# A reordered weave in a two-layer diffusion backbone: side work set at other places among the projections

## The chip, the cores and the metric

One core of a Trainium2 chip runs the whole program. The metric is device time in microseconds, the median of several executions.

## The reference

Two layers work on 512 latent tokens and 256 context tokens of width 1024, all in float32. Cut to what matters:

```python
for l in range(2):
    hl = rms_norm(xl, norm1_g[l]) * (1 + sc1) + sh1        # sh1, sc1, ... from silu(c) @ ada_w (adaLN)
    p = h @ w_in[l]                                        # one wide projection, split into parts
    att = window_attention(rope(q), rope(k), v, kc, vc, sink)
    mls = mlstm_output(mlstm_bidir(...), o_pre, ml_g)      # 4 heads, chunks of 128, both directions
    hy  = hyena_operator(dwconv(u), hyena_filters(...))    # filters: two sine layers; two long convolutions
    y   = sum(sigmoid(gate_r) * (branch_r @ w_branch[r]) for r in range(3)) @ w_out[l]
    xl  = xl + g1 * y
    xl  = xl + g2 * conv_ffn(rms_norm(xl, norm2_g[l]) * (1 + sc2) + sh2)   # D_FF 2816, width-3 conv, SiLU gate
    # the context tokens go the same way in layer 0 only
return rms_norm(xl, final_g)
```

## The kernel before, in words

All activations are kept with channels on the 128 partitions and tokens along the row; a part is the 512 latent columns or the 256 context columns. Each float32 product is made of three: weights and activations are split into a high and a low half (`split`, L340: ScalarE casts the high half, VectorE subtracts to get the low half), and `kstep` (L404) issues high x high, high x low and low x high into one PSUM tile. A weight tile of 128x1024 comes by a DMA from SP's queue (`raw`, L391) and is split (`weight`, L396); there are four slots for raw tiles and three for each split half (`WB = (4, 3)`). `proj` (L421) is one unit: a weight tile against all eight k-blocks of the normalised activations `hlh`, `hll`.

The projections are the backbone. Between their k-steps, `tick` (L358) gives each lane a credit: the planner's cost of the k-step times the lane's rate. A lane is a Python generator that emits a few instructions and yields their cost; it is stepped while its credit is positive. So the yields and the rates (`RATE`, one set a layer) decide where in the program a side step stands among the projections. `finish` (L379) runs what is left of the lanes at the end of a stage, with no projections between. The framework then orders each engine's queue by priority, which is program order unless `high_priority` or `manual_schedule` says otherwise, and by when it expects operands; every engine takes its queue in that order.

Stages of a layer, each with its own pools of tiles (`SIZES`: so many wide T tiles, so many 512-column H tiles):
- A: the first three projections (`proj_first`, L425), the mLSTM gate projection, then branch gates (`gate_proj`, L1530; `NG1` says up to which). Lanes: in layer 0 the hyena filters (`filters`, L627: per length two sine layers, `sin_of` L607, then taps and their transform), the mLSTM gate scans (`ml_gates`, L1287). In layer 0 `start` (L1681) comes first: DMAs of the input, adaLN products, the norm of the latent half; TensorE keeps program order there.
- mix: attention projections, then mLSTM projections (`ml_proj`, L1231) with the attention lane (`att_mix`, L1083), then the hyena projections (`hy_proj`, L895, which write `hyd` to DRAM) with the mLSTM lane (`ml_mix`, L1390: per head `prep`, L1400, and `chain`, L1430, whose last part normalises a head, transposes it (L1512) and stores it).
- E: the remaining gates and the merges (L1564), with the hyena lane (`hy_mix`, L957). `hy_start` (L974) reads channels of `hyd` back, folds them (`fold`, L904: DMA, then VectorE's sum L913 and difference L914), transposes them (`fold_tok`, L918, line L924) and splits them. `hy_body` (L989) runs the two convolutions of a half of the channels, kt by kt: load a spectrum tile `g` (L1012), products `pu` (L1020), `pair_products` (L927), accumulation (L1038, L1045). The x1 channels are folded at its beginning; the next half's start is stepped in the second convolution.
- ffn: the out-projection (`out_proj`, L1599; its last `NTAIL` units run part by part), a norm, up projections in threes at first, then pairs, and a down projection (`down`, L1620) one chunk behind; `residual` (L1592, executed at L1595) adds into x. The norm of the second part is put into `deferred` and emitted by `run_deferred` (L451). `KEEP` says how many units of the last but one down projection wait until the last up projections are out.

adaLN vectors that are needed later come from the lane `ada_rows` (L516), two VectorE products a row block at L528 for layer 0.

## Time and profile before

| | us |
|---|---|
| median of three runs | 2725.51 (2724.69 to 2727.54) |
| the profiled execution | 2729.28 |
| its span | 2727.2 |
| TensorE matmuls busy | 2584.6 |
| VectorE busy | 1860.9 |
| ScalarE busy | 1040.8 |
| GpSimd busy | 249.3 |

The span runs from the first to the last instruction of the profiled execution. Matmuls are pipelined, so a matmul's own duration is longer than its share of the queue; what counts is whether TensorE stands still. The stages by time: A of layer 0 up to about 303 us, attention to 540, mLSTM to 690, hyena and merges to 983, out-projection and FFN to 1640; layer 1: A to 1765, attention to 1985, mLSTM to 2100, hyena and merges to 2300, then the out-projection, the FFN and the final norm.

### The profile page before, as it was taken

Reading aid. Unit: us, or ns where it says so; the run is one execution under the profiler, and the core shown is the slowest. Engines: PE = TensorE matmul, PEld = TensorE weight load, DVE = VectorE, ACT = ScalarE, POOL = GpSimd, SP = SyncE. Lnnn points to the kernel's source line nnn. Section 1 sums busy time; section 2 is a strip of 40 time slices with the busy share of each in tenths; the row PEclk is TensorE's granted clock in tenths of the full one; section 3 lists DMA queues with packets and bytes.
Section 4 is the critical chain, followed back from the end, with each engine's and each line's share of the span. In section 5 each row is a group of like instructions: output and inputs, shape, how many; then the busy total and the mean of one; then the engine's idle time right before and its main releaser. Section 6 shows DMA issues by size and latency. Waiting matters only on the chain. (4 is left out here: it accounts for less than half of the span.)

```text
span 2727.2 us, 37870 instructions
## 1 busy us (share of the span) xinstructions
PE 2584.6 (95%) x14434; PEld 2192.3 (80%) x14434; DVE 1860.9 (68%) x3349; ACT 1040.8 (38%) x1875; POOL 249.3 (9%) x277
## 2 busy tenths in 40 slices
PE   6998999999998898999999998999998989999998
PEld 2887888788887787888888887877887778888887
DVE  6775676687568756877877667766376577666656
ACT  5344344455222224433333235444354233533333
POOL 3221110000000201110110001310000002000000
PEclk9999999999999798999999999999999999999999
DMA  7434532323557431334433225553335565233331
GB/s 265 122 118 129 163 102 70 91 94 112 190 175 273 146 109 45 116 118 113 113 117 106 77 59 196 181 132 99 92 123 177 182 211 187 78 93 101 93 101 62
DMA packets 155461, 349.99 MB, mean 128 GB/s; under 512 B 15809, under 2 KB 53166, under 8 KB 155152
## 3 DMA queue, kind: packets, MB, share of 16 engines
q1 hardware_dynamic: 135280, 322.18, 36.7%
q0 software_dynamic: 20000, 25.40, 3.9%
q8 instruction: 114, 1.87, 0.3%
q14 instruction: 67, 0.55, 0.1%
HBM read 288.59 MB, written 52.17 MB: 125 GB/s over the span
## 5 line engine op out<-in xcount | busy, mean ns | idle before, releaser
L407 PE MATMUL pg<-hh,wh 128*128 128x512 f32 (+1 forms) x2536 | 919.1, 363 | 12.7 <-ACT hh L342 7.7
L407 PE MATMUL pg<-hlo,wh 128*128 128x512 f32 (+1 forms) x2536 | 904.4, 357 | 2.7 <-DVE hlo L343 2.6
L407 PE MATMUL pg<-hh,wl 128*128 128x512 f32 (+1 forms) x2536 | 901.7, 356 | 0.1
L407 PEld LDWEIGHTS pg<-hh,wh 128*128 128x128 f32 x2536 | 485.5, 192 | 79.6 <-ACT hh L342 8.7
L342 ACT CAST wh<-wr 128x1024 fp32r<-128x1024 f32 x294 | 308.8, 1051 | 614.2 <-PE pg L407 580.4
L407 PEld LDWEIGHTS pg<-hlo,wh 128*128 128x128 f32 x2536 | 485.4, 191 | 64.8 <-DVE hlo L343 4.5
L407 PEld LDWEIGHTS pg<-hh,wl 128*128 128x128 f32 x2536 | 484.2, 191 | 65.3 <-issue 2.1
L343 DVE TENSOR_TENSOR wl<-wr,wh 128x1024 fp32r<-128x1024 f32 x294 | 363.6, 1238 | 204.5 <-ACT wh L342 200.1
L1595 DVE SCALAR_TENSOR_TENSOR x<-pg,mod,x 128x512 f32<-128x512 f32 (+1 forms) x242 | 148.9, 629 | 103.7 <-PE pg L407 96.5
L407 PE MATMUL pg<-fh,wh 128*128 128x512 f32 (+1 forms) x544 | 193.6, 357 | 11.2 <-DVE x L1595 10.5
L407 PE MATMUL pg<-fl,wh 128*128 128x512 f32 (+1 forms) x544 | 191.2, 352 | 0.0
L407 PE MATMUL pg<-fh,wl 128*128 128x512 f32 (+1 forms) x544 | 190.2, 350 | 0.9 <-DVE wl L343 0.9
L806 ACT ACTIVATE u<-pg,sv 128x512 f32<-128x512 f32 (+1 forms) x165 | 116.3, 707 | 122.5 <-PE pg L407 122.4
L807 DVE SCALAR_TENSOR_TENSOR u<-pg,sv,u 128x511 f32<-128x511 f32 (+1 forms) x165 | 108.4, 659 | 73.4 <-ACT u L806 72.8
L528 DVE SCALAR_TENSOR_TENSOR wr<-wr,silb 128x1024 f32<-128x1024 f32 x80 | 100.1, 1252 | 40.0 <-DMA wr<-in_adat 39.5
L407 PEld LDWEIGHTS pg<-fh,wh 128*128 128x128 f32 x544 | 103.4, 190 | 28.8 <-DVE x L1595 13.2
L407 PE MATMUL pg<-bh,wh 128*128 128x512 f32 (+1 forms) x320 | 114.5, 389 | 4.4 <-ACT bh L342 3.8
L407 PEld LDWEIGHTS pg<-fh,wl 128*128 128x128 f32 x544 | 103.4, 190 | 15.2 <-DVE wl L343 1.4
L407 PEld LDWEIGHTS pg<-fl,wh 128*128 128x128 f32 x544 | 103.6, 191 | 14.3 <-issue 0.7
L808 DVE SCALAR_TENSOR_TENSOR u<-pg,sv,u 128x511 f32<-128x511 f32 (+1 forms) x165 | 108.6, 660 | 2.2
L1136 ACT ACTIVATE p<-s,sm 128x512 f32<-128x512 f32 (+2 forms) x80 | 55.2, 690 | 127.6 <-DVE sm L1133 97.4
L407 PE MATMUL pg<-bh,wl 128*128 128x512 f32 (+1 forms) x256 | 97.2, 380 | 0.0
(321 smaller groups left out, 4043.9 us busy)
## 6 DMA issues: line engine op xcount, KB each, us to landing
wr<-in_wA SPq DMA_DIRECT2D x222, 512.0 KB
wr<-in_adat SPq DMA_DIRECT2D x80, 512.0 KB
wr<-in_wD SPq DMA_DIRECT2D x48, 512.0 KB
wr<-in_wB SPq DMA_DIRECT2D x24, 512.0 KB
gates<-gt SPq DMA_DIRECT2D x28, 384.0 KB
gc<-in_g POOLq DMA_DIRECT2D x40, 256.0 KB, 3.2
g<-gd SPq DMA_DIRECT2D x40, 256.0 KB
g<-gates SPq DMA_DIRECT2D x24, 384.0 KB
```

Of the source, the lines that this page charges most:

```text
L342: nc.scalar.copy(h, src)
L343: (nc.gpsimd if pool else nc.vector).tensor_tensor(l, src, h.bitcast(F32), op=ALU.subtract)
L407: self.nc.tensor.matmul(ps[:, :hi - lo], a[:, ks], b[:, lo:hi], start=(first and i == 0), stop=(last and i == 2))
L528: nc.vector.scalar_tensor_tensor(prod, aw, 1.0, self.silb[:, v, :], op0=ALU.mult, op1=ALU.mult, accum_out=self.mod[l][:, b * 4 + c, v:v + 1])
L806: nc.scalar.activation(dst[:, lo:hi], ps[:, :n], AF.Identity, bias=b, scale=w(1))
L807: V(dst[:, lo + 1:hi], ps[:, 0:n - 1], w(0), dst[:, lo + 1:hi], op0=mul, op1=add)
L808: V(dst[:, lo:hi - 1], ps[:, 1:n], w(2), dst[:, lo:hi - 1], op0=mul, op1=add)
L1136: nc.scalar.activation(t[:, :w], src, AF.Exp, bias=sm[:, 2 + j:3 + j], scale=0.125, accum_out=sm[:, 4 + j:5 + j])
L1595: self.nc.vector.scalar_tensor_tensor(x[m][:, lo:hi], ps[:, :hi - lo], self.mod[l][:, p * 8 + m, j:j + 1], x[m][:, lo:hi], op0=ALU.mult, o ...
```

## The change

- `filters` loses its sine layers to a generator `features`, which steps both lengths in turn. In layer 0 its first ten steps are emitted ahead of everything at high priority, two more behind the first adaLN product, the rest behind the first half of the norm; the filter lane is spawned after the eighth k-step of the first projections (`START` goes).
- `chain` ends with the last recurrence; the rest of a head becomes `tail`, which `ml_mix` steps at every even step of the next head's chain. The last tail yields its costs twice.
- `hy_start` folds the x1 channels too, for all halves before the first transposes, and yields 8.0 behind the folds at the beginning and 0.5 otherwise (2.0 before); the next start is stepped at the end of the first convolution as well. The E pool gets a 28th H tile.
- `att_mix` yields 4.0 before its first item.
- `NTAIL` 2 to 3; in the FFN `run_deferred` is called after k-step 3 (layer 0) or 1 (layer 1) of the first part (`MID`); the first three projections always go k by k together.
- `KEEP` of layer 0 goes from 0 to 4, `NG1` of layer 1 from 11 to 13, the adaLN lane of layer 0 from 1/12 to 1/8; rates of layer 1: mlg 0.616 to 0.7, att 1.008 to 0.84, ml 2.5 to 1.75, hy 2.149 to 1.1.

```diff
--- before.py
+++ after.py
@@ -240,22 +240,22 @@
 
 
 class Prog:
-    NG1 = (18, 11)
+    NG1 = (18, 13)
     NG2 = (18, 16)
-    RATE = ({'filt': 1.587, 'ada': 1.362, 'mlg': 0.55, 'att': 0.92, 'ml': 1.258, 'hy': 0.997}, {'filt': 0.389, 'ada': 0.512, 'mlg': 0.616, 'att': 1.008, 'ml': 2.5, 'hy': 2.149})
-    SIZES = {'A0': (18, 23), 'A1': (8, 38), 'mix': (20, 19), 'E': (16, 27), 'ffn0': (20, 21), 'ffn1': (28, 0)}
+    RATE = ({'filt': 1.587, 'ada': 1.362, 'mlg': 0.55, 'att': 0.92, 'ml': 1.258, 'hy': 0.997}, {'filt': 0.389, 'ada': 0.512, 'mlg': 0.7, 'att': 0.84, 'ml': 1.75, 'hy': 1.1})
+    SIZES = {'A0': (18, 23), 'A1': (8, 38), 'mix': (20, 19), 'E': (16, 28), 'ffn0': (20, 21), 'ffn1': (28, 0)}
     BOUNDS = ((0, 2, 4, 6, 8, 10, 12, 14, 16, 18, 22), (0, 4, 8, 12, 16, 20, 22))
-    START = (0.8,)
     FILL = (6.0, 6.0, 6.0)
     SQP = ((), (0, 1, 2, 3, 4, 5, 6, 7))
     AHEAD = 50
     EARLY = True
-    KEEP = (0, 2)
+    KEEP = (4, 2)
+    MID = (3, 1)
     TAKE = 50
     FADDS = 7
     WB = (4, 3)
     FINP = (1, 4)
-    NTAIL = 2
+    NTAIL = 3
@@ -294,7 +294,7 @@
         self.A = {(l, i): c.tile([P, KD, 2], F32, name=f"A{l}{i}") for l in range(DEPTH) for i in (1, 2)}
         self.sil = c.tile([P, KD, 32], F32, name="sil")
         self.silb = c.tile([P, 2, D], F32, name="silb")
-        self.g_dram = {}
+        self.g_dram, self.feat = {}, {}
 
     def load_consts(self):
         nc, a = self.nc, self.a
@@ -422,9 +422,12 @@
         w = self.weight(self.a["wA"][l, m])
         return list(self.gemm(w, 0, self.hlh, self.hll, parts))
 
-    def proj_first(self, l, ms, parts, hooks=None):
-
-
+    def proj_first(self, l, ms, parts, hooks=None, mid=None):
+
+
+        hooks = dict(hooks or {})
+        if mid is not None:
+            hooks[mid] = self.run_deferred
         raws = self.early or [None] * 3
         self.early = None
         ws = [self.weight(self.a["wA"][l, m], raw=r) for m, r in zip(ms, raws)]
@@ -433,15 +436,15 @@
             one = [self.G() for _ in ms]
         outs = [[] for _ in ms]
         for i, (lo, hi, _) in enumerate(parts):
-            if i:
+            if i and mid is None:
                 self.run_deferred()
             pss = [ps[:, lo:hi] for ps in one] if joint else [self.G() if i == 0 else self.M() for _ in ms]
-            for group in ((0,), (1,), (2,)) if i else ((0, 1, 2),) if hooks else ((0, 1), (2,)):
+            for group in ((0,), (1,), (2,)) if i else ((0, 1, 2),):
                 for k in range(KD):
                     for j in group:
                         self.kstep(pss[j], ws[j], slice(k * P, k * P + P), self.hlh[k], self.hll[k], lo, hi, k == 0, k == KD - 1)
                     self.tick(3 * len(group) * max(0.109, (hi - lo) * 0.422e-3))
-                    if i == 0 and hooks and k in hooks:
+                    if i == 0 and k in hooks:
                         hooks[k]()
             for o, ps in zip(outs, pss):
                 o.append((lo, hi, ps))
@@ -451,8 +454,8 @@
     def run_deferred(self):
         for f in self.deferred:
             f()
-        for rate, gen in self.late:
-            self.spawn(rate, gen)
+        for rate, *gens in self.late:
+            self.spawn(rate, *gens)
         self.deferred, self.late = [], []
 
     def parts(self, l, ctx=None):
@@ -624,17 +627,25 @@
         nc.scalar.activation(out, a, AF.Sin)
         yield 1.0
 
-    def filters(self, l, L, resident, overlap):
-
+    def features(self, l, lengths):
+
+        gens = [self.feature(l, L) for L in lengths]
+        while gens:
+            for g in list(gens):
+                c = next(g, None)
+                if c is None:
+                    gens.remove(g)
+                else:
+                    yield c
+
+    def feature(self, l, L):
         nc, a = self.nc, self.a
         s = "5" if L == SEQ else "2"
-        nT = L // P
         zt = self.H("zt")
         nc.sync.dma_start(zt[0:33, :L], a["z" + s])
         w12 = self.H("w12")
         nc.sync.dma_start(w12[0:33, 0:64], a["hw1"][l])
         nc.sync.dma_start(w12[0:64, P:2 * P], a["hw2"][l])
-        dec, gc = {}, {}
         h = zt
         yield 0.1
         for i, (kk, m) in enumerate(((33, 64), (64, P))):
@@ -649,7 +660,15 @@
         nc.scalar.copy(hd[0:64, :L], h[0:64, :L])
         nc.vector.tensor_tensor(hd[64:128, :L], h[64:128, :L], hh[64:128, :L].bitcast(F32), op=ALU.subtract)
         yield 1.5
-        dec = {}
+        self.feat[l, L] = hd
+
+    def filters(self, l, L, resident, overlap):
+
+        nc, a = self.nc, self.a
+        s = "5" if L == SEQ else "2"
+        nT = L // P
+        hd = self.feat[l, L]
+        dec, gc = {}, {}
         if resident:
             for t in range(nT):
                 dec[t] = self.H("dec")
@@ -959,9 +978,10 @@
 
         need = l < DEPTH - 1
         st = {}
-        yield from self.hy_start(l, SEQ, (0,), st)
-        yield from self.hy_body(l, SEQ, 0, st, out, self.hy_start(l, SEQ, (1,), st))
-        yield from self.hy_body(l, SEQ, 1, st, out, self.hy_start(l, CTX, (0, 1), st) if need else iter(()))
+        for c in self.hy_start(l, SEQ, (0,), st, 8.0):
+            yield c
+        yield from self.hy_body(l, SEQ, 0, st, out, self.hy_start(l, SEQ, (1,), st, 0.5))
+        yield from self.hy_body(l, SEQ, 1, st, out, self.hy_start(l, CTX, (0, 1), st, 0.5) if need else iter(()))
         lanes = [self.hy_body(l, CTX, half, st, out, iter(())) for half in range(2)] if need else []
         while lanes:
             for g in list(lanes):
@@ -971,13 +991,17 @@
                 else:
                     yield c
 
-    def hy_start(self, l, L, halves, st):
+    def hy_start(self, l, L, halves, st, wait):
         nJ = L // 2 // P
         if L not in st:
             st[L] = self.hy_consts(L)
+        base = 0 if L == SEQ else SEQ
+        folded = []
         for half in halves:
-            fv = self.fold(0, half, 0 if L == SEQ else SEQ, L)
-            yield 2.0
+            folded.append(self.fold(0, half, base, L))
+            st[L, half, "x1"] = self.fold(1, half, base, L)
+            yield wait
+        for half, fv in zip(halves, folded):
             sd = st[L, half] = []
             for j in range(nJ):
                 pt = self.fold_tok(fv, L // 2, j)
@@ -994,7 +1018,7 @@
         d = st[L]
         sd = st.pop((L, half))
         W3 = lambda a, b: ((a[0], b[0]), (a[0], b[1]), (a[1], b[0]))
-        f1 = self.fold(1, half, base, L)
+        f1 = st.pop((L, half, "x1"))
         hx1 = []
         for o in range(2):
             if o == 0:
@@ -1052,7 +1076,7 @@
                     nc.scalar.copy(x, pt)
                     hx1.append(x)
                 yield 1.8
-                if o == 1:
+                if o == 1 or kt == nK:
                     c = next(nxt_start, None)
                     if c is not None:
                         yield c
@@ -1197,6 +1221,7 @@
 
         n = len(items)
         at = lambda i: items[i] if 0 <= i < n else None
+        yield 4.0
         for i in range(n + 3):
             a0, a1, a2 = at(i), at(i - 1), at(i - 2)
             if a0:
@@ -1395,7 +1420,7 @@
         outs = list(range(6)) if need else list(range(4))
         nch = len(outs)
         q1, q2, mn, dcb = ml["q1"], ml["q2"], ml["mn"], self.dcb
-        prepared = {}
+        prepared, tails = {}, []
 
         def prep(h):
             while len(ml["q"]) <= h:
@@ -1429,7 +1454,7 @@
 
         def chain(h):
             q = ml["q"][h]
-            nm, rc = [self.T("nm", [P, 6, 129]) for _ in range(2)], []
+            nm = [self.T("nm", [P, 6, 129]) for _ in range(2)]
             orders = ([4, 5, 0, 1, 2, 3], [5, 4, 3, 2, 1, 0])
             C = [None, None]
             pend = []
@@ -1478,6 +1503,9 @@
                         pend.append((d, c, i, pu))
                     yield 0.9
             finish()
+            tails.append(tail(h, nm))
+
+        def tail(h, nm):
             hs = self.T("hs", [P, 6, P])
             for d in range(2):
                 r = d * 32 + h
@@ -1519,13 +1547,16 @@
         yield from prep(0)
         for h in range(4):
             nxt = prep(h + 1) if h < 3 else iter(())
+            last = tails.pop() if tails else iter(())
             for i, c in enumerate(chain(h)):
                 yield c
-                if i % 2:
-                    x = next(nxt, None)
-                    if x is not None:
-                        yield x
+                x = next(nxt if i % 2 else last, None)
+                if x is not None:
+                    yield x
+            yield from last
             yield from nxt
+        for x in tails.pop():
+            yield 2 * x
 
     def gate_proj(self, l, dst, ms, first=None):
         nc = self.nc
@@ -1650,7 +1681,7 @@
                     self.residual(l, 5, m, x)(lo, hi, j, self.gemm_part(w, (m % per) * nk * P, fh, fl, lo, hi)[2])
 
         todo = None
-        first = self.proj_first(l, (M_UP, M_UP + 1, M_UP + 2), fine)
+        first = self.proj_first(l, (M_UP, M_UP + 1, M_UP + 2), fine, mid=self.MID[l])
         for c in range(len(bounds) - 1):
             for i in range(bounds[c], bounds[c + 1]):
                 gv = []
@@ -1678,7 +1709,7 @@
             todo = c
         down(todo, True)
 
-    def start(self, xd):
+    def start(self, xd, feat):
 
         nc = self.nc
         lat, cx = self.parts(0)
@@ -1693,6 +1724,8 @@
         self.early = [self.raw(self.a["wA"][0, m]) for m in (M_MO, M_MO + 1, M_MO + 2)]
         aw[3] = self.ada_load(3, [self.T("aw")[:, :512] for _ in range(KD)])
         p0 = self.ada_products(aw[0])
+        for _ in range(2):
+            next(feat)
         sums = [self.square_sums(x, lo, hi, self.SQP[j]) for lo, hi, j in self.parts(0)]
         rs = self.rstd_of(sums)
         p2 = self.ada_products(aw[2])
@@ -1704,6 +1737,8 @@
         for k in low:
             self.hlh[k], self.hll[k] = self.HL("hh"), self.HL("hlo")
         self.norm_part(0, 1, x, lat, rs[0], low, ts)
+        for _ in feat:
+            pass
         p1 = self.ada_products(aw[1])
         self.ada_take(0, 1, p1)
         p3 = self.ada_products(aw[3])
@@ -1735,13 +1770,19 @@
                 if l == 0:
                     nc.sync.dma_start(self.sv[0], a["sv"][0])
                     self.ada_prepare()
-                    self.spawn(R["filt"], self.filters(0, SEQ, True, True), self.filters(0, CTX, True, True))
+                    feat = self.features(0, (SEQ, CTX))
                     with tc.high_priority(1000):
-                        self.tick(self.START[0])
+                        for _ in range(10):
+                            next(feat)
                     inorder = ExitStack()
                     inorder.enter_context(tc.manual_schedule(engines={mybir.EngineType.PE}))
-                    hooks = self.start(xd)
-                    hooks[KD - 1] = inorder.close
+                    hooks = self.start(xd, feat)
+
+                    def begun():
+                        inorder.close()
+                        self.spawn(R["filt"], self.filters(0, SEQ, True, True), self.filters(0, CTX, True, True))
+
+                    hooks[KD - 1] = begun
                 else:
                     hooks = None
                     xc = [Two(None, self.H("xc")) for _ in range(KD)]
@@ -1759,7 +1800,7 @@
                 self.finish("A")
                 if l == 0:
                     self.silu_rows()
-                    self.spawn(1 / 12, self.ada_rows(0, range(4, 12)), stays=True)
+                    self.spawn(1 / 8, self.ada_rows(0, range(4, 12)), stays=True)
             with tc.tile_pool(name=f"mix{l}", bufs=1) as self.mp:
                 self.nT, self.nH = self.SIZES["mix"]
                 with self.psum(5) as self.pm:
@@ -1807,7 +1848,7 @@
                 self.out_proj(l, x, second)
                 if need:
                     self.spawn(1 / 28, self.ada_rows(1, range(0, 4)))
-                    self.late.append((self.RATE[1]["filt"], self.filters(1, SEQ, False, False)))
+                    self.late.append((self.RATE[1]["filt"], self.features(1, (SEQ,)), self.filters(1, SEQ, False, False)))
                 for k in range(KD):
                     self.dump(f"xa{l}", x[k][:, :n], (slice(None), k))
                 if need:
```

## Rows read from the trace of the kernel before

**Rows 1.** The page: TensorE's busy time, and the granted clock in 40 slices.

```profile
PE 2584.6 (95%) x14434; PEld 2192.3 (80%) x14434; DVE 1860.9 (68%) x3349; ACT 1040.8 (38%) x1875; POOL 249.3 (9%) x277
...
PEclk9999999999999798999999999999999999999999
```

**Rows 2.** Windows: length; PE, PEld, DVE, ACT, POOL busy; clock; DMA; GB/s.

```profile
53.00:73.00 20.00, 13.44 (x53) 10.10 (x52) 9.22 (x17) 6.62 (x11) 3.88 (x3) 0.83 0.00 0
...
204.00:221.00 17.00, 10.26 (x48) 9.12 (x47) 6.31 (x18) 5.71 (x8) 0.00 (x0) 0.70 0.26 94
...
702.00:716.00 14.00, 11.26 (x61) 9.25 (x61) 6.51 (x13) 2.11 (x5) 0.00 (x0) 0.88 0.86 302
...
826.00:841.00 15.00, 10.04 (x54) 9.12 (x53) 13.83 (x27) 5.55 (x8) 0.00 (x0) 0.77 0.61 202
...
849.00:878.00 29.00, 27.29 (x170) 23.67 (x168) 21.32 (x45) 5.09 (x8) 2.55 (x2) 1.00 0.79 270
...
904.00:952.00 48.00, 40.66 (x173) 34.43 (x173) 31.62 (x62) 9.49 (x22) 12.86 (x12) 0.68 0.55 182
...
1046.00:1090.00 44.00, 36.16 (x163) 29.47 (x162) 34.82 (x59) 22.94 (x43) 8.45 (x8) 0.81 0.13 40
...
1660.00:1676.00 16.00, 10.22 (x62) 9.12 (x62) 15.63 (x22) 10.13 (x15) 4.76 (x4) 0.79 0.17 51
...
1748.00:1762.00 14.00, 11.12 (x52) 9.03 (x51) 9.36 (x20) 8.49 (x14) 0.77 (x1) 0.76 0.56 170
...
1797.00:1824.00 27.00, 22.36 (x120) 17.84 (x119) 20.79 (x37) 10.94 (x22) 6.87 (x15) 0.94 0.58 157
...
2109.00:2124.00 15.00, 9.09 (x36) 7.23 (x35) 4.87 (x8) 2.05 (x4) 0.53 (x1) 0.77 0.93 314
...
2193.00:2207.00 14.00, 7.85 (x39) 6.45 (x40) 8.40 (x15) 4.35 (x8) 3.46 (x2) 0.88 0.62 199
...
2341.00:2366.00 25.00, 19.58 (x126) 17.84 (x125) 16.57 (x38) 15.40 (x36) 3.58 (x5) 0.86 0.14 43
```

**Rows 3.** Timeline of the opening: start, duration, instruction, idle before and its releaser.

```profile
37.59 1.28 ACT L624 ACT_TABLE_LOAD   x1
...
54.47 2.14 DVE L620 SCALAR_TENSOR_TENSOR sa<-sq,sa 128x512 f32<-128x512 f32 x3
...
59.48 0.79 PE L711 MATMUL pm<-w3h,hd 128*128 128x512 f32 x1 [5.47 <-ACT w3h L342]
...
212.36 1.22 PE L642 MATMUL pm<-hsin,w 64*128 64x256 f32 x2 [4.75 <-ACT hsin L624]
```

**Rows 4.** Waits of PE, mLSTM stages: total us, times, longest.

```profile
PE pm L1512 <- DVE hs L1503: 6.6, 4, 2.4
PE pg L407 <- DVE u L808: 1.9, 1, 1.9
...
PE pm L1512 <- DVE hs L1503: 4.6, 4, 1.4
PE pg L407 <- DVE u L808: 2.1, 2, 1.1
```

**Rows 5.** Hyena stage: adaLN products (groups by line), spectra waits and loads.

```profile
L528 DVE SCALAR_TENSOR_TENSOR wl<-wr,silb 128x1024 fp32r<-128x1024 f32 x11 | 14.2, 1291 | 14.8 <-PE pg L407 14.8
L528 DVE SCALAR_TENSOR_TENSOR wr<-wr,silb 128x1024 f32<-128x1024 f32 x11 | 13.9, 1268 | 0.1
...
DVE t L934 <- DMA g<-gd: 17.6, 12, 2.5
...
g<-gd SPq DMA_DIRECT2D x40, 256.0 KB
```

**Rows 6.** The page: the two casts of a weight tile.

```profile
L342 ACT CAST wh<-wr 128x1024 fp32r<-128x1024 f32 x294 | 308.8, 1051 | 614.2 <-PE pg L407 580.4
...
L343 DVE TENSOR_TENSOR wl<-wr,wh 128x1024 fp32r<-128x1024 f32 x294 | 363.6, 1238 | 204.5 <-ACT wh L342 200.1
```

**Rows 7.** Timeline of VectorE at the seam into layer 1.

```profile
1663.55 1.76 DVE L587 TENSOR_TENSOR nx<-x,rstd 128x512 f32<-128x512 f32 x1
...
1665.83 0.47 DVE L1595 SCALAR_TENSOR_TENSOR x<-pg,mod,x 128x256 f32<-128x256 f32 x1
```

## The prediction

> **What bounds the kernel now.** I read the page's busy times first. TensorE (PE) is busy for 2584.6 of 2727.2 us, VectorE for two thirds of that [rows 1]. So the span is TensorE's own work plus about 142 us in which it stands still, plus what the clock costs: around its stops the granted clock falls to the lower of two levels, 1.2 of 2.4 GHz, and the matmuls there take twice as long. The clock line shows where: at the end of the first hyena stage it falls to 7 tenths [rows 1]. The change touches hardly any matmul; it only moves steps. So I looked for each place where TensorE waits, with a table of stretches: stretch minus PE busy is standing time, and (1 - granted clock) times PE busy is what the low clock costs on top. The stretch 53 to 73 us, for instance, gives 6.56 + 0.17 x 13.44 = 8.8 us [rows 2]. The view of waits, stage by stage, gives what each wait was for, and the timeline shows the chain behind it. "Loss" below is this sum for a stretch of [rows 2].
>
> A tuned order stays an order: each engine takes its instructions in a row that was fixed beforehand, by priority (program order) and expected readiness. A transpose that comes up before its input is there stops every projection behind it. That is what the change attacks: it sets consumers later than the chains that feed them.
>
> **The change part by part.** Ends of the bounds are in brackets.
>
> (a) Sine layers in the opening. Before, the last sine layer is finished so late that the first filter matmul stands 5.47 us for its weights [rows 3]; the stretch loses 8.8. After it, the filters start behind the first eight k-steps, with the sines done. But the second sine layers of both lengths, eight VectorE and three ScalarE instructions each, now lie ahead of the second half of the norm: three of the eight take 2.14 us [rows 3], twice that for all eight is my estimate, and the smaller context layer comes on top; in the context's own stretch VectorE is busy for 6.31 us altogether [rows 2]. Much of it fits where VectorE waits for DMAs, not all. I take 4 us of new delay: gain 4.8 [2.3 to 8.8]. The sine of layer 1 moves ahead of the logarithm's table, so ScalarE reloads its table once more, 1.28 us [rows 3], in the time when the input is still landing: nothing. The Trainium skill (ScalarE: Activation LUTs, What ACT_TABLE_LOAD costs) speaks against such mixing: it counts about 2.66 us a switch, the load and a drain. In the trace the next activation begins as the load ends, so I keep 1.28; by the page (a) would be 1.4 us worse.
>
> (b) The context's sine layers leave the filter lane. There TensorE waited for the hidden layer, 4.75 us, with nothing in front of it [rows 3]; the stretch loses 6.74 + 3.1 = 9.8. The chain is gone from there: 9.8 [7 to 9.8].
>
> (c) mLSTM tails in the next head. Four transposes per layer wait for the normalised heads, 6.6 and 4.6 us, and the convolutions behind them hold back evacuations for 1.9 and 2.1 us [rows 4]: 15.2 in all. Woven into every second step of the next chain, each tail has a head's worth of projections in front of its transposes. The last tail's steps count twice: by the yields in the code layer 0 then needs 116.7 units, at 1.258 a unit of clock 92.8 of the stage's 93.6, so it just fits. Layer 1, at 1.75 instead of 2.5, needs 58 of 62 instead of 38. Gain 12.5 [6 to 15].
>
> (d) The first fold of a hyena stage. Transposes come up before hyd has been read back: losses 2.74 + 1.35 = 4.1 and 5.91 + 2.1 = 8.0 (stretches 702 and 2109). The yield of 8.0 for 2.0, and the rate 1.1 for 2.149 in layer 1, move them about 6 units of projection clock, some 6 us, back. That covers 2.74 and just covers 5.91: 10 [4 to 12].
>
> (e) Later folds, issued half a convolution earlier, with the x1 folds beside them: 826 loses 4.96 + 2.3 = 7.3, 849 loses 1.7, 2193 loses 6.15 + 0.9 = 7.1. At 826 the fold stood in VectorE's queue, which is full there (13.83 of 15 us [rows 2]); earlier issue helps only if the H slots are there. 11.5 of 16.1 [3 to 16].
>
> (f) The end of hyena in layer 0. The stretch 904 to 952 loses 7.34 + 13 = 20.3, the largest of all. Its rate isn't changed, and hyena ends as late as before (136.5 of 140.4 units, against 135). What helps: the adaLN rows of layer 0 run at 1/8 instead of 1/12 and are done before; 22 products of 1.27 to 1.29 us leave VectorE in this stage [rows 5], in proportion some four of them in this stretch. 3 [-6 to 10].
>
> (g) Norm seams. 1046 loses 7.84 + 6.9 = 14.7, 2341 loses 5.42 + 2.7 = 8.2. Three out-projection units instead of two cover the first part's norm, and the second part's norm is issued after the fourth (second) k-step of the first projections instead of after all. A cost: there are three slots of split weights, so the third weight of the next stage waits until the tail releases one; its casts take 1.05 and 1.24 us [rows 6], at three seams 0 to 7 us. I take 15.5 - 3 = 12.5 [2 to 22].
>
> (h) Two gate projections more in the second A stage, and the gate lane at 0.7: it needs 31.8 / 0.7 = 45 of 52 units where it needed 52 of 41.5. The stretch 1748 loses 2.88 + 2.7 = 5.6: 5 [2 to 5.6].
>
> (i) Attention starts 4 units later. In layer 1 that covers the copies it waited for (1797 loses 4.64 + 1.3 = 6.0); at 0.84 it ends at 97.5 of 98.6 units. In layer 0 four units more are left to the end of the stage: 4.5 - 1 = 3.5 [-1 to 6].
>
> (j) Four units of a down projection held back at the end of the first FFN. The loss of 7.9 at 1660 isn't a lack of cover: VectorE works on the norm (one multiplication takes 1.76 us), and the residual for which TensorE waits stands behind it in the queue [rows 7]. That stays: 0 [-2 to 3].
>
> Sum: 4.8 + 9.8 + 12.5 + 10 + 11.5 + 3 + 12.5 + 5 + 3.5 + 0 = 72.6 us. None of these moves is free of a new order elsewhere. The seams that already had two units of cover still lose 8 and 15 us, so I subtract a fifth, 15 us, for waits that come up in new places: net 58. The profiled execution took 2729.3 us, 2.1 more than its span; it would become 2671. It stands 3.8 above the median of the runs, so the median becomes 2725.5 - 58 = 2667.5.
>
> **The rivals.**
>
> Covers that only shift. The chain is late by the trace's clock, not the planner's; a consumer moved back meets the next late chain, and only (b) and half of (c) stay. For it: VectorE is busy for 21.32 of 29 and 13.83 of 15 us in stretches of the hyena stage [rows 2], so every move lengthens some queue. Against it: most waits have one cause, seen by name. Gain 6 to 20, about 2712.
>
> Slots: slower. In the hyena stages the early x1 folds hold two H tiles more, four more for the context's two halves, and the pool grows by one. The spectra loads (g, 40 in all [rows 5]) need a slot to start. VectorE already waits for them, 17.6 us in 12 waits, at most 2.5 [rows 5]. If every one of the 40 comes 2.5 us late with no projection to cover it, that is 100 us: 2725.5 - 73 + 100 = about 2753. It decides for slower from some 1.9 us exposed per load. Against: layer 0 has gate projections and two merges as cover. A sentence of the Trainium skill (Perfetto Trace Analysis, Optimization Strategy) reads alike: the same gap over and over can mean that there is no room for the next tile. No such row of equal gaps is in the trace of before.
>
> Nothing moves. The order is made by readiness as well as priority; if the planner puts the same matmuls in the same places, the time stays within 0.2%. Against: yields and rates are large changes to the program order.
>
> All covered. Every loss above goes, the end of hyena too, with no new waits: 95 and more, below 2630.
>
> **How the numbers follow.** Forecast (gain 20 to 95) 0.70; covers shift 0.13; slots 0.07; nothing moves 0.04; all covered 0.06. The forecast is likeliest: 2667. For eight times in ten I go from 2630 to 2712, the forecast's own ends and most of the first rival. A measurement tells about 0.2%, 5.5 us, from no change: faster 0.70 + 0.13 + 0.06 = 0.89, same 0.04, slower 0.07.
>
> **What would show it.** Right: TensorE busy unchanged, standing time down from 142 to about 100 us; no wait for hsin inside the filters; hs and the first fold gone from the top of the list of waits; seams with the clock at full. The end of layer 0's hyena and the residual wait at the end of the first FFN should still be there. Wrong: waits of g or fold of equal size along both hyena stages (slots); a first filter matmul much later than 59.5 us [rows 3]; last tails or attention steps running alone at the end of their stages.

## The result, and the profile after

| | before | after |
|---|---|---|
| median, us | 2725.10 (2722.46 to 2727.54) | 2686.03 (2678.02 to 2690.41) |
| ratio | 1 | 0.9853, 95% interval 0.9826 to 0.9881 |
| profiled execution, its span, us | 2729.28, 2727.2 | 2689.34, 2687.6 |
| span less TensorE busy, us | 142.6 | 123.3 |

The change makes the kernel 39 us faster. The forecast was a gain of 58 us, to 2667. The direction and the range held; the measured gain is a third smaller than the forecast.

Three lines of the page after, which answer to [rows 1]: busy times, then the granted clock.

```profile
span 2687.6 us, 37927 instructions
...
PE 2564.3 (95%) x14458; PEld 2181.9 (81%) x14458; DVE 1854.0 (69%) x3350; ACT 1034.1 (38%) x1871; POOL 253.3 (9%) x277
...
PEclk8999999999999999999999999999999999999999
```

The hole of 7 tenths at the end of the first hyena stage is gone from the clock line, and an 8 stands at its very start, where TensorE now waits longer for the opening (clock 0.87 up to the first projection, 1.00 before). TensorE's own busy time fell by 20.3 us although the work is the same, because a matmul at the lower clock level counts as busy for longer: behind a stop at 2084.6 us of after, matmuls of 512 columns start 0.43 us apart at 1.2 GHz, and then 0.23 us apart at 2.4 GHz. So half of the gain is the clock, and half is time in which TensorE no longer stands still (142.6 to 123.3).

To see where, I cut both traces at the same instructions: the first projection matmul, the first copy of a `k` part, the last copy of `mq` (end of the attention projections), the last convolution of the hyena projections, the first matmul on `yh` (start of the out-projection), the last on `fh` (end of the FFN); the second layer likewise, with the last matmul on `yh` besides. The windows of after (columns as in [rows 2]):

```profile
0.00:51.95 51.95, 22.43 (x92) 6.55 (x93) 39.02 (x76) 23.15 (x37) 20.86 (x26) 0.87 0.86 318
51.95:306.94 254.99, 240.03 (x1381) 206.22 (x1378) 163.30 (x301) 99.94 (x164) 46.73 (x47) 0.97 0.40 127
...
522.72:682.88 160.16, 155.41 (x1000) 135.16 (x999) 132.02 (x347) 85.52 (x203) 1.04 (x2) 0.99 0.37 119
682.88:958.73 275.85, 260.59 (x1603) 232.50 (x1601) 186.29 (x362) 76.25 (x152) 35.23 (x39) 0.97 0.53 179
958.73:1654.24 695.51, 676.04 (x3837) 588.76 (x3836) 499.06 (x770) 242.36 (x334) 57.88 (x56) 0.99 0.34 102
...
1960.18:2060.71 100.53, 99.69 (x560) 84.08 (x559) 80.44 (x225) 59.97 (x124) 0.00 (x0) 1.00 0.39 130
2060.71:2262.25 201.54, 187.95 (x986) 158.65 (x985) 138.30 (x241) 59.71 (x105) 26.14 (x24) 0.97 0.60 200
...
2307.88:2674.71 366.83, 364.16 (x1712) 305.45 (x1711) 233.15 (x313) 139.36 (x197) 4.45 (x6) 1.00 0.29 89
```

In before, the first two of these and layer 0's hyena and merges are:

```profile
0.00:43.77 43.77, 23.16 (x86) 6.18 (x86) 29.43 (x51) 19.69 (x29) 19.97 (x26) 1.00 0.95 351
43.77:308.43 264.66, 241.65 (x1363) 206.65 (x1363) 174.25 (x323) 106.27 (x173) 46.39 (x47) 0.95 0.40 126
...
686.04:979.51 293.47, 272.96 (x1602) 239.44 (x1601) 213.08 (x407) 76.77 (x152) 36.28 (x39) 0.93 0.55 185
```

The next table sets these stretches beside those of before and of the experiments (lengths in us; a column's name is that of the run in the sections below):

| stage | before | after | opening_before | tails_inline | att_now | folds_before | ada_12 | undo_rest | seams_before | rates_1 | best2 |
|---|---|---|---|---|---|---|---|---|---|---|---|
| up to the first projection | 43.8 | 52.0 | 43.6 | 51.5 | 52.9 | 51.3 | 52.0 | 51.1 | 52.1 | 51.6 | 45.2 |
| A, layer 0 | 264.7 | 255.0 | 264.4 | 257.8 | 252.3 | 252.2 | 255.7 | 255.9 | 254.8 | 251.9 | 259.0 |
| attention projections, 0 | 213.7 | 215.8 | 218.4 | 215.2 | 214.4 | 215.3 | 216.6 | 215.7 | 214.3 | 215.7 | 214.5 |
| mLSTM and hyena projections, 0 | 163.9 | 160.2 | 161.2 | 168.6 | 153.8 | 160.2 | 156.4 | 156.4 | 161.3 | 160.1 | 153.7 |
| hyena and merges, 0 | 293.5 | 275.9 | 277.0 | 277.0 | 276.6 | 280.3 | 281.6 | 294.6 | 277.0 | 275.1 | 272.8 |
| out-projection and FFN, 0 | 697.2 | 695.5 | 694.9 | 695.0 | 695.3 | 695.8 | 695.0 | 690.3 | 699.0 | 696.0 | 693.0 |
| A and attention, 1 | 308.2 | 305.9 | 305.2 | 306.3 | 306.1 | 307.0 | 302.9 | 305.1 | 306.1 | 310.2 | 305.4 |
| mLSTM and hyena projections, 1 | 108.3 | 100.5 | 100.3 | 104.0 | 100.9 | 100.5 | 100.5 | 103.9 | 100.7 | 100.6 | 100.5 |
| hyena and merges, 1 | 202.9 | 201.5 | 201.4 | 200.8 | 201.8 | 205.7 | 200.6 | 203.6 | 202.2 | 202.8 | 200.6 |
| FFN, 1 | 372.9 | 366.8 | 366.8 | 366.8 | 366.8 | 366.8 | 366.8 | 366.8 | 373.0 | 366.8 | 366.8 |
| median of the runs | 2725.1 | 2686.0 | 2691.2 | 2702.7 | 2681.5 | 2692.5 | 2687.9 | 2702.6 | 2697.4 | 2693.3 | 2671.8 |

A column is one profiled execution. A stage that an edit doesn't touch differs by 1 to 4 us between columns, layer 0's A by up to 6 (251.9 to 257.8); differences of that size are not read unless a wait in the trace goes with them. A ratio is taken against the kernel before in the same round of runs, whose median lay between 2722.3 and 2726.3 us, so small differences are read from ratios and not from medians. The gains of after: 17.6 us in layer 0's hyena, 7.8 and 6.1 us in layer 1's mLSTM and FFN, 9.7 in A of which 8.2 were lost just before it, and small change elsewhere.

### The profile page after: what moved, and what is told of

Its sections match the earlier page's. It is cut to its first block, busy times and chain, and to the rows that moved or that the text cites. A ratio compares the mean times of both kernels' runs of the same rounds, so it can differ in the third digit from the quotient of the medians.

```text
span 2687.6 us, 37927 instructions
## 1 busy us (share of the span) xinstructions
PE 2564.3 (95%) x14458; PEld 2181.9 (81%) x14458; DVE 1854.0 (69%) x3350; ACT 1034.1 (38%) x1871; POOL 253.3 (9%) x277
## 5 line engine op out<-in xcount | busy, mean ns | idle before, releaser
L1626 DVE SCALAR_TENSOR_TENSOR x<-pg,mod,x 128x512 f32<-128x512 f32 (+1 forms) x243 | 148.7, 627 | 100.7 <-PE pg L407 94.0
L407 PEld LDWEIGHTS pg<-fh,wl 128*128 128x128 f32 x544 | 103.7, 191 | 15.1 <-DVE wl L343 1.4
L407 PEld LDWEIGHTS pg<-fl,wh 128*128 128x128 f32 x544 | 104.0, 191 | 14.0 <-issue 0.7
L1156 DVE TENSOR_REDUCE sm<-s 128x1 f32<-128x512 f32 (+2 forms) x80 | 55.2, 690 | 56.0 <-PE s L1142 37.1
```

Source lines behind the costliest of these rows:

```text
L407: self.nc.tensor.matmul(ps[:, :hi - lo], a[:, ks], b[:, lo:hi], start=(first and i == 0), stop=(last and i == 2))
L1156: nc.vector.tensor_reduce(sm[:, j:j + 1], src, axis=AX.X, op=ALU.max)
L1626: self.nc.vector.scalar_tensor_tensor(x[m][:, lo:hi], ps[:, :hi - lo], self.mod[l][:, p * 8 + m, j:j + 1], x[m][:, lo:hi], op0=ALU.mult, o ...
```

## The experiments

Line numbers from here on are those of after: `chain`'s old tail is at L1531 and L1540, the folds at L930 to L943, the residual at L1626.

**The opening.** The timeline of after shows why the first projection starts 8.2 us later (ScalarE, then TensorE; idle before and its releaser in brackets):

```profile
37.78 2.16 ACT L342 CAST hh<-nx 128x512 fp32r<-128x512 f32 x4
39.96 1.28 ACT L627 ACT_TABLE_LOAD   x1
41.56 0.63 ACT L627 ACTIVATE hsin<-sa 128x512 f32<-128x512 f32 x1 [0.31 <-DVE sa L625]
42.10 2.92 ACT L342 CAST wh<-wr 128x1024 fp32r<-128x1024 f32 x3
44.97 0.42 ACT L627 ACTIVATE hsin<-sa 128x256 f32<-128x256 f32 x1
...
46.93 0.58 ACT L501 COPY adae<-adap 128x512 f32<-128x512 f32 x1
...
47.56 1.12 PE L504 MATMUL adaq<-ident,adae 128*128 128x128 f32 x4 [13.15 <-ACT adae L501]
```

The sine layers and their casts stand in ScalarE's queue ahead of a 0.58 us copy of an adaLN product; TensorE, held to program order there, can't reach its first projection before that copy, and stands 13.15 us for it, 3.1 in before. Behind the opening, in A of layer 0, the waits of TensorE in the filter lane were these in before (its own line numbers), and are these in after:

```profile
PE pm L711 <- ACT w3h L342: 5.8, 2, 5.5
PE pm L720 <- POOL ab L707: 5.4, 7, 1.8
PE pm L642 <- ACT hsin L624: 4.7, 1, 4.7
```

```profile
PE pm L739 <- POOL ab L726: 8.4, 7, 1.8
PE pm L730 <- ACT w3h L342: 3.6, 3, 1.9
```

opening_before puts the sine layers back where they were:

```diff
...
-                    feat = self.features(0, (SEQ, CTX))
-                    with tc.high_priority(1000):
-                        for _ in range(10):
-                            next(feat)
+                    self.spawn(R["filt"], self.features(0, (SEQ,)), self.filters(0, SEQ, True, True),
+                               self.features(0, (CTX,)), self.filters(0, CTX, True, True))
+                    with tc.high_priority(1000):
+                        self.tick(0.8)
...
```

> The changed kernel with the opening of the kernel before: the sine layers are again part of the filter lane, which is spawned first. This measures parts (a) and (b) alone. My prediction said 14.6 us; the stage times of the two profiles say 1.5, since the first projection starts 8.2 us later and the filters win back 9.7. Theory (stage times): start at 43.8 us, the A stage of layer 0 ends within 3 us of the changed kernel's, median 2686 to 2690. Rival (the sum of the prediction): 2698 to 2701. The wait for hsin inside the filter lane, 4.75 us, must be back in either case.

2691.18 us (ratio 0.9875, 0.9851 to 0.9900): 5 us slower than after, with an interval that overlaps after's. By stages, the projections begin 8.4 us earlier and A takes 9.4 longer, with the wait for `hsin` (4.8 us) back in it. The two nearly cancel.

sines_last keeps the sine layers out of the filter lane, but sets what is left of them behind that copy:

```diff
-        for _ in feat:
-            pass
+        for _ in range(2):
+            next(feat)
         p1 = self.ada_products(aw[1])
...
             self.norm_part(0, 1, x, cx, rs[1])
+            for _ in feat:
+                pass
```

> The changed kernel, but the second sine layers are no longer emitted ahead of the last adaLN products: only their first three VectorE instructions stand there, the rest comes behind the context's norm. Theory (the copy of the third adaLN product stands in ScalarE's queue behind the sines and the weight casts, and TensorE, in program order there, stands 13.15 us for it): the first projection starts at about 44 us instead of 52.0, as before the change, and all later stages follow some 7 to 8 us earlier; median about 2678. Rival (the opening is bound by the input's DMAs, which now land behind the sine tables' loads): the start stays at 51 to 52 us and the time within 2 us of 2686.

2683.00 us (0.9852, 0.9832 to 0.9872). The first projection starts at 44.9 us, so the cause of the delay is settled. The time hardly follows: A then took 258.6 us, 3.6 more than in after, and by the ratio nothing is won (0.9852 against 0.9853).

**The mLSTM tails.** "The weave" below is the tail of a head stepped within the next head's chain. tails_inline runs a head's tail right behind its own chain again. It is not quite the order of before, where the next head's preparation was stepped along with the tail; here what is left of that preparation comes behind it.

```diff
-            last = tails.pop() if tails else iter(())
...
-                x = next(nxt if i % 2 else last, None)
-                if x is not None:
-                    yield x
-            yield from last
-            yield from nxt
-        for x in tails.pop():
-            yield 2 * x
+                if i % 2:
+                    x = next(nxt, None)
+                    if x is not None:
+                        yield x
+            yield from tails.pop()
+            yield from nxt
```

> The changed kernel with the mLSTM tails back behind their own chains, rates as changed. Theory (part (c): the transposes wait for hs): the waits of the transposes for hs come back, 3 to 7 us a layer, the mLSTM stages take 3 to 5 us more in layer 0 and 4 to 8 us more in layer 1, median 2693 to 2699. Rival (the lower rate of layer 1 did it, not the weave): layer 0 loses 3 to 4, layer 1 under 2 us.

2702.74 us (0.9922, 0.9902 to 0.9943): 16.7 us slower than after, 8.4 in layer 0's stage, about twice what was expected, and 3.5 in layer 1's. Its waits, of the first and the second layer's stage (total, times, longest), are close to those of [rows 4] again:

```profile
PE pm L1540 <- DVE hs L1531: 5.5, 4, 2.4
...
PE pm L1540 <- DVE hs L1531: 4.2, 3, 1.5
```

In after they are 0.8 and 0.5. Layer 1 gained 7.8 us, of which the weave gives 3.5. undo_rest (below), which keeps the weave and has the old rate of 2.5, takes 103.9 us there: the slower rate gives 3.3.

**The attention yield.** att_now takes the one line `yield 4.0` out of `att_mix`.

> The changed kernel without the yield of 4.0 ahead of the attention's first item. Theory (the yield made the wait of the second item's scores for the first softmax longer, 4.3 and 4.7 us instead of 1.5 in both layers): both attention stages take 2 to 3 us less (215.8 to about 213.5 in layer 0; layer 1 303 for 305.9), median 2681. Rival (prediction, part i): layer 1 loses 3 to 4.5 us as its wait for the stacked copies comes back, layer 0 gains 1; median 2688 to 2690.

2681.47 us (0.9841, 0.9823 to 0.9860). The ratio alone doesn't separate it from after, but the stages do: layer 0's mLSTM stage falls from 160.2 to 153.8 us (153.7 in best and best2, which have the edit too), and nothing else moves by more than the spread. In after, the end of attention and the start of the first mLSTM head run with no projections between them:

```profile
544.63 1.08 PE L1212 MATMUL po<-pT,vt 128*64 128x256 f32 x6 [0.55 <-DVE pT L1198]
546.23 1.60 PE L1434 MATMUL pm<-mq,mk 128*128 128x128 f32 x12 [0.52 <-ACT o L1219]
...
551.13 0.46 PE L1493 MATMUL pu<-vt,dt 128*128 128x129 f32 x2 [1.88 <-DVE dt L1452]
...
552.68 0.46 PE L1493 MATMUL pu<-vt,dt 128*128 128x129 f32 x2 [0.87 <-DVE dt L1452]
```

Without the yield none of the four waits is there: 3.8 us of the 6.4, and the rest is TensorE's busy time (155.4 to 152.8 us). So the median came out at the expected 2681 by luck: the theory put the gain into the attention stages, by a shorter wait for the first softmax, but that wait is 4.2 us in layer 0 without the yield and 4.3 with it, and those stages gained 1.4 and nothing. Why it is longer than the at most 1.5 us of before stays open.

In layer 1 the yield exchanges one wait for another. The waits in A and attention of layer 1, in att_now and then in after:

```profile
PE s L1130 <- DMA x<-xl: 3.4, 2, 1.9
PE s L1130 <- ACT p L1160: 2.1, 1, 2.1
```

```profile
PE s L1130 <- ACT p L1160: 4.7, 1, 4.7
PE s L1130 <- DMA x<-xl: 1.1, 1, 1.1
```

The copies from DRAM are mostly covered, and the softmax is waited for instead: 5.5 us in all without the yield, 5.8 with it.

**The first fold.** In layer 1 the wait for the first fold went from 5.91 [rows 2] to 6.1 us. wait24 yields 24.0 there instead of 8.0 (layer 0 keeps 8.0).

```diff
-        for c in self.hy_start(l, SEQ, (0,), st, 8.0):
+        for c in self.hy_start(l, SEQ, (0,), st, 8.0 if l == 0 else 24.0):
```

> The changed kernel, but the first hyena start of layer 1 yields 24.0 behind its folds instead of 8.0. In the order of TensorE's queue the first four transposes of that stage stand behind the 8437th projection matmul both before the change and after it; the yield of 8.0 didn't move them. At 24.0 the first two stand behind the 8454th. Theory (the place was set by when the operand was expected, and only a yield beyond that moves it): 17 matmuls of 0.228 us are 3.9 us, so the wait of 6.1 us at the first transposes falls to about 2, and the stage from the last convolution to the first output unit takes 3 to 5 us less than 201.5. Rival (the wait follows the loads, which move along): the wait stays at 5 to 6 us and the stage at 200 to 203.

2687.94 us (0.9861, 0.9842 to 0.9880): nothing won, and 204.5 us for the stage instead of 201.5. First the transposes of after, then those of wait24:

```profile
2084.57 1.09 PE L943 MATMUL pm<-ident,fold 128*128 128x128 f32 x4 [6.14 <-issue]
```

```profile
2080.56 0.58 PE L943 MATMUL pm<-ident,fold 128*128 128x128 f32 x2 [2.14 <-issue]
2084.69 0.48 PE L943 MATMUL pm<-ident,fold 128*128 128x128 f32 x1 [3.12 <-DVE fold L932]
```

Counted through TensorE's queue, the first four transposes stand behind the 8437th projection matmul both before and after; three times the yield moves them 17 matmuls on, some 4 us, and only splits the wait. So their place isn't set by the yield alone; as the order goes by priority and by expected operands, the second is what is left. That it expects them too early because of the load is argued, not shown: the 256 KB load of the first fold is slow. In after it is issued at 2074.0 us and VectorE's sum starts at 2083.9 (the same 10 us as before: 2105.8 to 2116.2):

```profile
L930 SPq DMA_DIRECT2D u<-hyd x4: 430/444/792, 2074.0 to 2092.2; - x4
L932 DVE TENSOR_TENSOR fold<-u x3: 419/421/426, 2083.9 to 2092.0; 128x256 f32<-128x256 f32 x3
```

**The later folds and the adaLN lane.** folds_before puts `hy_start` and the x1 folds back, with 27 H tiles:

```diff
...
-            folded.append(self.fold(0, half, base, L))
-            st[L, half, "x1"] = self.fold(1, half, base, L)
-            yield wait
-        for half, fv in zip(halves, folded):
+            fv = self.fold(0, half, 0 if L == SEQ else SEQ, L)
+            yield 2.0
...
-        f1 = st.pop((L, half, "x1"))
+        f1 = self.fold(1, half, base, L)
...
-                if o == 1 or kt == nK:
+                if o == 1:
```

> The changed kernel with the hyena's folds as before: yield 2.0 behind each fold, x1 folded at the beginning of each half's body, the next start stepped in the second convolution alone, 27 H tiles. Theory 1 (early folds gave layer 0's hyena stage its 17.7 us): that stage goes from 275.8 back to 287 to 293 us; layer 1's by 0 to 3 us. Theory 2 (the adaLN products that left VectorE gave it): under 5 us in either layer.

2692.52 us (0.9878, 0.9858 to 0.9898): 4.5 and 4.2 us more in the two hyena stages. Layer 1's 4.2 hangs on the new rate too: with the old folds and the old rate (undo_rest) that stage takes 203.6. ada_12 puts only the adaLN lane back (1 / 8 to 1 / 12):

> The changed kernel with the adaLN lane of layer 0 at 1/12 again, so that some 22 of its 64 products lie in the hyena stage of layer 0 once more. Theory 2 (those products held up the end of hyena): the stage goes from 275.8 to 285 to 293 us, and the earlier stages take 0 to 2 us less. Theory 1 (early folds): it stays within 4 us of 275.8. If each gives about half, both theories hold in part.

2687.86 us (0.9864, 0.9841 to 0.9887): 5.7 us more in layer 0's hyena, 3.7 less in the mLSTM stage ahead of it, where the lane's products now stand less dense. undo_rest puts both back, and `KEEP` at (0, 2), ml at 2.5 and hy at 2.149:

> The changed kernel with the folds, the adaLN lane (1/12), KEEP (0) and layer 1's rates of mLSTM (2.5) and hyena (2.149) as before, so that each stage shows its own part. Layer 0's hyena stage: folds alone cost 4.5 us and the adaLN lane alone 5.8 us when undone; if they add, it takes 286 us, if they cover for each other it goes to 291 to 294, as before the change. Out-projection and FFN of layer 0: KEEP was put at nothing, so 695.5 within 1.5 us. mLSTM stage of layer 1: the weave alone gave 3.5 of 7.8 us; if the lower rate gave the rest, 104 to 105 us. Hyena stage of layer 1: with the folds undone it took 205.7; if the lower rate is what costs there, it falls to about 203, as before the change.

2702.61 us (0.9916, 0.9902 to 0.9931), and 294.6 us for layer 0's hyena: 18.7 more than after, where the two alone cost 4.5 and 5.7. So neither of the two theories holds by itself, and the third does: each edit covers for the other. The last stretch of the stage, in undo_rest, folds_before, ada_12 and after (before: 904 to 952 in [rows 2], clock 0.68):

```profile
896.00:944.00 48.00, 40.62 (x177) 34.47 (x176) 33.31 (x65) 10.21 (x24) 12.87 (x12) 0.69 0.50 162
```

```profile
884.00:932.00 48.00, 42.13 (x230) 35.27 (x229) 38.67 (x71) 11.89 (x27) 17.64 (x16) 0.93 0.48 156
```

```profile
884.00:932.00 48.00, 41.09 (x223) 35.41 (x224) 39.23 (x69) 10.32 (x23) 20.68 (x18) 0.90 0.50 160
```

```profile
884.00:932.00 48.00, 43.48 (x251) 36.78 (x250) 37.84 (x70) 12.68 (x29) 19.21 (x18) 0.96 0.49 168
```

TensorE stands 7.4 us in undo_rest's row and 4.5 to 6.9 in the others: at most a few us less. The rest is the clock, 0.69 against 0.90 and more. A mean of 0.69 between full and half speed says that the clock was low for some 30 of the 48 us; in the other rows it was for 4 to 10. It falls behind short stops in all four. Which of the stops keep it low in undo_rest isn't shown: ada_12 stands nearly as long, 6.9 us, and has 0.90.

**The norm seams.** seams_before: `NTAIL` 2, `MID` (None, None), and the third of the first projections behind the other two again.

```diff
-    MID = (3, 1)
+    MID = (None, None)
...
-    NTAIL = 3
+    NTAIL = 2
...
-            for group in ((0,), (1,), (2,)) if i else ((0, 1, 2),):
+            for group in ((0,), (1,), (2,)) if i else ((0, 1, 2),) if hooks else ((0, 1), (2,)):
```

> The changed kernel with two out-projection units in the tail instead of three, the second part's norm emitted behind the first part of the first projections, and those projections two and one. Theory (part (g), as the stage times give it): layer 0's stretch from the out-projection to the end of the FFN loses 2 us, layer 1's 6 us; median about 2694. Rival (the prediction's 12.5 us): 2698 or more, with the wait for the second norm, 3.8 us, back at both seams.

2697.39 us (0.9901, 0.9876 to 0.9925): 11.4 slower, of it 3.5 in layer 0's FFN stage and 6.2 in layer 1's. The old wait for the normalised rows is back at both seams:

```profile
PE pm L407 <- ACT hh L342: 3.8, 1, 3.8
...
PE pg L407 <- ACT hh L342: 3.9, 1, 3.9
```

In after other waits stand at layer 0's seam (waits from 959 to 1110 us):

```profile
PE pg L407 <- DVE wl L343: 3.7, 2, 2.7
PE pg L407 <- DVE hlo L343: 2.0, 1, 2.0
```

The first line is two waits: 0.92 us for the low half of one of the first three weights, and 2.74 for that of the weight behind them. The timeline shows what held up the second (ScalarE, VectorE, TensorE):

```profile
1055.71 1.05 ACT L342 CAST wh<-wr 128x1024 fp32r<-128x1024 f32 x1 [1.75 <-PE pm L407]
...
1057.36 1.20 DVE L531 SCALAR_TENSOR_TENSOR wl<-wr,silb 128x1024 fp32r<-128x1024 f32 x1
...
1059.10 1.21 DVE L531 SCALAR_TENSOR_TENSOR wr<-wr,silb 128x1024 f32<-128x1024 f32 x1
...
1060.85 1.21 DVE L343 TENSOR_TENSOR wl<-wr,wh 128x1024 fp32r<-128x1024 f32 x1
...
1062.11 0.80 PE L407 MATMUL pg<-hh,wl 128*128 128x512 f32 x1 [2.74 <-DVE wl L343]
```

The weight's high half is there at 1056.8 us. VectorE comes to its low half only at 1060.9, behind two adaLN products and steps of layer 1's sine layers.

**Gates and rates of layer 1.** rates_1 puts `NG1` at (18, 11), mlg at 0.616, att at 1.008, hy at 2.149.

> The changed kernel with layer 1's gate lane (0.616), attention (1.008), hyena (2.149) and the number of gate projections in the A stage (11) as before; the folds stay early. A and attention of layer 1: part (h) foresaw that the stretch loses 5 us again (305.9 to 311); the stage times say 2 to 3. Rival: nothing, within 1 us, because the attention's own wait is unchanged. Hyena stage of layer 1: if the lower rate was worth what part (d) and (e) foresaw, 201.5 goes to 207 or more; if the rate costs nothing and brings nothing, it stays within 1.5 us.

2693.30 us (0.9882, 0.9865 to 0.9899). A and attention of layer 1 take 310.2 us, 4.3 more than in after; the columns with the new attention rate lie between 302.9 and 307.0. A wait is back there that after doesn't have (before had 1.4 us there, and 1.5 beside it):

```profile
PE pm L1397 <- ACT q L1374: 2.8, 1, 2.8
```

Hyena takes 1.3 more, within the spread.

**Put together.** best has sines_last, att_now and a third try at the first fold: its loads go by GpSimd's queue, ahead of the stage's tables.

```diff
...
-            nc.sync.dma_start(u[:, :L], self.hyd[:, kind * 4 + half * 2 + i, base:base + L])
+            (nc.gpsimd if ahead else nc.sync).dma_start(u[:, :L], self.hyd[:, kind * 4 + half * 2 + i, base:base + L])
...
```

> The changed kernel with three repairs: the second sine layers behind the context's norm, no yield ahead of the attention, and the loads of the first fold of each hyena stage issued from GpSimd's queue ahead of the twelve transform tables. The first two gave 3 and 4.5 us alone. Theory for the third (the fold waits because its four loads are issued from SP's queue behind weight loads and share the DMA engines with 3 MB of tables): the transposes come earlier in TensorE's queue (behind matmul 8398 instead of 8437 in layer 1) and still wait under 2 us instead of 6.1, and the hyena stage takes 4 us less in layer 1 and 2 in layer 0; median 2672 to 2675. Rival (the order always puts them where the planner expects the load, and the load is later): the wait stays at 4 us or more, median 2678 to 2681.

2675.68 us (0.9821, 0.9807 to 0.9834). The fold's wait is 5.2 us in layer 0 and 4.1 in layer 1, where it was 3.5 and 6.1: the transposes came up earlier along with the loads, in layer 1 behind the 8398th projection matmul instead of the 8437th. The wait is as the rival had it, and the median lies between the two forecasts. The hyena stages take 277.5 and 200.6 us, within the spread of after's; that the gain is that of the other two edits (6.5 us up to the first projection, 6.4 in layer 0's mLSTM stage) is read from the stages, no run has these two alone. best2 leaves the loads alone and takes `KEEP` back to (0, 2):

> The changed kernel with three edits: the second sine layers of both filters placed as the last emissions of the opening's rows, behind the copy of the third adaLN product; the attention lane's yield back at none; and the feed-forward keep of (4, 2) back at (0, 2). Theory: the kept bundles only add the short wait of 1.23 us at layer 0's first norm seam, so its feed-forward stage goes from 695.5 us to 693 to 694.5, and the other stages stay as where the first two edits stand alone or with the hyena loads moved; median 2674 to 2677 us. Rival: the 690.3 us that this stage took where the keep, the rates and the two folds were put back together is the keep's alone; then the stage takes 690 to 691.5 us and the median is 2670 to 2673 us. Second rival: the moved hyena loads were what made the faster of the earlier runs; then the median without them is 2678 us or more.

2671.75 us (0.9805, 0.9788 to 0.9822), 13 us ahead of after by the ratios; it has the lowest median, but its interval overlaps best's. Layer 0's FFN stage is at 693.0 us, as the theory had it. It takes 695.5 in after, but 693.8 in best, which keeps the four units: `KEEP` is worth 2.5 us at most, 0.8 beside best, and not the 5 by which undo_rest came in under its expected 695.5. The waits for the residual in that stage come to 11.8 us in after, 10.7 in best2 and 10.2 in undo_rest. Most of the rest of undo_rest's 690.3 is low clock that didn't follow the same stops: TensorE is busy there for 672.3 us, for 676.0 in after, with the same matmuls. The stretch of the second norm part, in after and in undo_rest:

```profile
1057.00:1069.00 12.00, 9.26 (x39) 6.86 (x39) 10.15 (x18) 5.78 (x7) 0.00 (x0) 0.86 0.34 106
```

```profile
1071.00:1083.00 12.00, 9.26 (x53) 7.29 (x52) 11.71 (x21) 5.56 (x6) 0.00 (x0) 1.00 0.37 110
```

TensorE stands 2.74 us in both, ahead of the same matmul and for the same operand. In the one the clock falls and 39 matmuls fit, in the other it doesn't and 53 do.

The median lies in the rival's range all the same: layer 0's hyena stage took 272.8 us, which `KEEP` can't explain. Whether it is the spread stays open.

## Why the prediction was right or wrong

The direction was right because most of the named waits went: those for `hsin`, for `hs` and for the normalised rows. The gain fell short because new waits came and because some steps didn't move. By groups of parts, forecast and measured (stages of before less after): opening (a, b) 14.6 and 1.5; tails (c) 12.5 and 11.5; hyena (d, e, f) 24.5 and 19.0; seams (g, j) 12.5 and 7.4 (1.7, 6.1 and -0.3 for the out-projection of layer 1); second A and attention (h, i) 8.5 and 0.2. Together 72.6 and 39.6: 33 us are missing where 15 had been set aside.

- **(a, b) failed in two terms.** "I take 4 us of new delay" was 8.2: the estimate counted VectorE's eight instructions and overlooked what else stood in ScalarE's queue behind the sines. And the two losses in the filter lane, 18.6 us together, gave 9.7: the wait for `hsin` went, but that for `w3h` only fell from 5.8 to 3.6, in smaller pieces, and that for the next link of the same lane (`ab`) grew from 5.4 to 8.4. The first filter matmul, at 59.5 us before [rows 3], stands at 69.9 without a wait. That it comes much later than 59.5 was named as a sign of being wrong, and this is the first rival, in one place.
- **(c) held** in its mechanism; that the size fits is partly luck. The waits for `hs` nearly went. By the runs that undo it, the weave gives 8.4 and 3.5 us and layer 1's slower rate 3.3. Layer 0's stage shows only 3.7, since it also bears what (i) costs there, 6.4, and 3.7 of the denser adaLN lane. These three don't add up (8.4 less 10.1 would be a loss), so they overlap; how isn't shown. The stage of tails_inline is even 4.7 us longer than that of before.
- **(d) failed.** The yield of 8.0 was to move the transposes back by 6 us. They stayed behind the same matmul in layer 1, and the wait is 6.1 us for 5.9; in layer 0 it is 3.5 for 2.7. That readiness orders the queue as well as priority was named in the rival "nothing moves" and given 0.04 for the whole kernel; it should have been asked for each move by itself.
- **(e, f) came near in sum, for the wrong reason.** The forecast counted the adaLN products that leave VectorE rightly (213.1 to 186.3 us busy in the stage; 22 by 1.28 is 28) and priced their effect at 3 us, because it took the 20.3 us of [rows 2] as many waits, each to be repaired. It was mostly the clock: 13 of the 20.3 were lost to the low clock, beside 7 us of standing, and a partial repair gave back most of it; of the 17.6 us that the stage won, 12.4 are TensorE's busy time. "The end of layer 0's hyena should still be there" was wrong. Layer 1, where no such stretch was, gave 1.4 us for the 7.1 taken as its losses in (e).
- **(g) held for the norms, was too large in size, and had the wrong cost.** The old waits for the normalised rows went. The foreseen cost was that the third weight waits for a slot; what came at layer 0's seam is 2.0 us for the low half of the rows, 0.92 for that of a weight, and 2.74 for the weight behind the first three, which stood in VectorE's queue. The clock there is 0.88 (0.81 before) and not full. At layer 0's seam the stage won 1.7 us of a loss of 14.7 (3.5 by the undoing), at layer 1's 6.1 of 8.2.
- **(h) held**, as far as one execution shows: 4.3 of 5 by rates_1, 2.8 of it a wait that is seen by name. **(i) failed**: its own remark that four more units are left to the end of the stage in layer 0 was priced at 1 us; the run without the yield gives 6.4 there, since the leftover runs with no projections beside it ("steps running alone at the end of their stages" was another sign of being wrong). In layer 1 a softmax took its gain.
- **(j) held**: the residual's 4.5 us wait stays in after. The kept units added a residual wait of 1.2 us.
- The rival of late slots falls. The 17.6 us in 12 waits for `g` of [rows 5] are those of the whole kernel, 7.7 of it in layer 0's hyena stage; in after it is 7.2 there and 15.1 in 8 waits in the whole kernel (`DVE t L953 <- DMA g<-gd: 15.1, 8, 3.7`).
- "TensorE busy unchanged" was a wrong sign to look for: busy time holds the low clock. Standing time fell to 123 us, not to the 100 foreseen.
- The rule of the Trainium skill (ScalarE: Activation LUTs, What ACT_TABLE_LOAD costs), 2.66 us a switch, isn't borne out: in the timeline above, the activation behind the load begins 1.60 us after its start, 1.28 of it the load and 0.31 a wait for VectorE.

## What to carry to other kernels

Before a consumer is moved back, look in the trace at what fixes its place in the queue: a step that is ordered by expected readiness need not follow the program when a yield is changed. Before a chain is moved forward, list everything that then stands behind it on each engine, down to a copy of half a microsecond for which a strictly ordered engine waits. And split a stretch's loss into standing and low clock first: if the clock is most of it, one small repair may give most of it back, and a second little.

## What the runs showed that I had not expected

- Stops of 7 us in all, spread over 48 us, went with 13 us lost to the low clock, and of two partial repairs, each worth 13 to 14 alone, the second added only some 5. The same 2.74 us of standing went with a granted clock of 0.86 in one run and 1.00 in another, so a stage with the same waits can differ by a few us.
- A 256 KB load of `hyd`, issued while the DMA engines are nearly full (0.87 of their time in layer 1's stretch 2076 to 2091), takes 10 us until its consumer starts, in after as in before.
